# A chain of six layers on one core: gating taken in turn with the next block's top 16, H additions spread, a low rotary product on 128 rows

## The chip, the core and the metric

The kernel runs on one core of a Trainium2 chip. The core has a matrix engine (PE, with PEld for its weight loads), a vector engine (DVE), a scalar engine (ACT), GpSimd (POOL), a queue engine that only issues transfers (SP) and 16 DMA engines. The metric is the device time of one launch in microseconds, as the median of repeated runs: 3226.28 us over 3 runs before the change (3226.07 to 3231.53).

## The reference, cut to what matters

One sequence of 512 tokens (16 meta tokens ahead of it in the first layer) of width 1024, all in float32. The layers in order: a mixer (differential attention beside a gated recurrence), a PEER feed-forward layer, pooling, gated convolution, latent attention (MLA), pooling again, and a last norm. The change is in the mixer's loads, the PEER layer and the MLA layer.

```
# PEER, per block of 128 tokens
q = xb @ w_query                                   # 8 heads, two halves of 128
s = q . subkeys                                    # 128 scores per half
sv, si = top_k(s, 16)                              # "lists": per half the best 16
cand = sv[0][:, None] + sv[1][None, :]             # 256 pairs per head
top_s, pos = top_k(cand, 16)                       # "top 16": the best pairs
experts, gates = i*128 + j of pos, softmax(top_s)
hid = gelu(u_table[experts] . xb) * gates
y = sum of hid * v_table[experts]
# MLA, per head and block of 128 queries
s = (q_nope . k_nope + q_rope . k_rope) * scale, causal softmax, p @ v
```

## The kernel before, in words

Products in full precision are made of three f32r matmuls: each operand is split in a high part (`whi`, `xh`) and a low part (`wlo`, `xl`), and `mm3` (L146 to L149) adds high x high, high x low and low x high. So every weight tile of 128x1024 is loaded by SP (`load_w`, L135), cast to `whi` by ACT (L141) and subtracted to `wlo` by DVE (L143), and then used by 24 matmuls.

The PEER layer does not gather for its first 384 tokens: it computes all 16384 hidden values for them (128 tiles of the table u, 24 matmuls each with 384 columns), multiplies each by a dense gate that is zero for all but the 128 chosen experts, and multiplies with all of the table v (128 tiles again). The last 128 tokens are done by rows: one indirect transfer of POOL (L724) gathers one row of u or v per token, and DVE multiplies it (L737) or adds it (L745); there are 256 such row steps, made by the generator in the class `Few`, three of them fetched ahead.

`peer_early` runs first. For 16 tiles of w_query it makes the scores, and DVE picks the lists (`list_scores`, L788 to L792, in steps). `experts_x` (L799) then scales and splits the input of the u tiles (L803, L219, L220). After that 96 of the 128 u tiles run, one per iteration: `u_tile`, waiting transfers `outs`, the dense matmuls that the iteration before left in `pend`, a row step if one is due, and `some(SIDE)`, which takes steps from the front of the list `side` until their written costs use up SIDE. The list holds DVE work: the rest of the lists, `topk` for the four token blocks (block 3 first, since its experts feed the row steps), and `all_gates`, which builds dense gates for a block of 128 tokens. Gates are made for 8 tokens at a time: two DVE operations of 2048 columns (`oh` L973, `og` L975), 16 small matmuls (L983), and two ACT copies (L986) into `stg`. A `stg` tile holds 32 tokens; there are two of them. When it is full, four transfers of 512 KB to `g_d` are put in `outs`. An iteration issues one of these (L1019), and the function `gates` issues all that wait when it starts on the next 32 tokens (L961, L962). ACT issues them in its own order of work.

`peer_late` runs the other 32 u tiles and all 128 v tiles. It reads the gates back (`get_gates`, L1067), the weighted hidden values are made by DVE (L1054) and split, and `slot` hands out the 208 row steps that are left by a rate per kind of tile (FEW_RATE). A v pass over 8 tiles adds into four PSUM tiles; at its end four DVE additions (L1116) put them into H.

In the MLA layer `unit_a` makes 128 rows of scores of one head by four matmuls: two passes of `qn` x `kn` in float32 (L1458), the f32r product of the stacked rotary query with the high part of the rotary key (L1459), and the product of its high half, 64 rows, with the low part of the key (L1460). The stacked query holds 64 rows of high part and 64 rows of low part, the key's tiles hold the same 64 rows twice. There are 64 such units.

The order of work on each engine inside the PEER layer is the order of the code (`manual_schedule`); engines only wait for each other by semaphores.

## Time and profile before

| | before |
|---|---|
| median of 3 runs | 3226.28 us |
| the profiled execution | 3233.49 us, span 3231.8 us |
| granted PE clock, mean | 0.986 |
| PE busy | 3133.5 us (97%) |
| DVE busy | 2195.7 us (68%) |
| ACT busy | 1191.6 us (37%) |
| POOL busy | 550.1 us (17%) |

Busy time is the time in which an engine has an instruction running. Matmuls overlap in the records, so the mean time of one matmul is longer than the distance to the next: counts over a stretch give the pace. Times of rows are microseconds from the start of the span. In the rows, `mm` is a PSUM tile, `hid` the hidden values of one u tile (one per iteration, so its records mark the iterations), and `row` a gathered row tile.

### The profile page before, as it was taken

Reading aid. Unit: us, or ns where it says so; the run is one execution under the profiler, and the core shown is the slowest. Engines: PE = TensorE matmul, PEld = TensorE weight load, DVE = VectorE, ACT = ScalarE, POOL = GpSimd, SP = SyncE. Lnnn points to the kernel's source line nnn. Section 1 sums busy time; section 2 is a strip of 40 time slices with the busy share of each in tenths; the row PEclk is TensorE's granted clock in tenths of the full one; section 3 lists DMA queues with packets and bytes.
Section 4 is the critical chain, followed back from the end, with each engine's and each line's share of the span. In section 5 each row is a group of like instructions: output and inputs, shape, how many; then the busy total and the mean of one; then the engine's idle time right before and its main releaser. Section 6 shows DMA issues by size and latency. Waiting matters only on the chain.

```text
span 3231.8 us, 42341 instructions
## 1 busy us (share of the span) xinstructions
PE 3133.5 (97%) x16233; PEld 2715.0 (84%) x16233; DVE 2195.7 (68%) x3887; ACT 1191.6 (37%) x1793; POOL 550.1 (17%) x490
## 2 busy tenths in 40 slices
PE   8999999889899999999999999999999999999998
PEld 7787879889899999999988888888888777778886
DVE  5466689989757888888887565544446656666664
ACT  3334323365654233333343223222224444443222
POOL 2121100111114653433350001000002000010001
PEclk9999989999999999999999999999999999999999
DMA  3211225777889999999962333323232222223231
GB/s 115 72 59 33 92 66 175 243 223 242 275 275 327 356 335 353 358 351 341 340 247 92 93 97 93 95 93 97 93 98 65 72 58 71 72 80 96 92 98 65
DMA packets 194395, 525.03 MB, mean 162 GB/s; under 512 B 17040, under 2 KB 71568, under 8 KB 194064
## 3 DMA queue, kind: packets, MB, share of 16 engines
q1 hardware_dynamic: 88128, 300.18, 28.6%
q0 software_dynamic: 38144, 136.33, 11.8%
q10 hardware_dynamic: 67920, 85.82, 7.8%
q8 instruction: 127, 2.08, 0.3%
q14 instruction: 76, 0.62, 0.1%
HBM read 474.03 MB, written 46.14 MB: 161 GB/s over the span
## 4 chain that ended last, share of the span: by engine, by line
PE 66%; issue 15%; DVE 8%; POOL 5%; DMA 4%; ACT 2%; ACTq 0%; POOLq 0%; DVEq 0%
PE mm L147 20%; PE mm L149 19%; PE mm L148 19%; POOL row L724 4%; DMA row<-in_v_rows_dram,gi 2%; DVE wlo L143 2%; DMA hh<-hid_d 1%; PE mm L1491 1%; PE mm L1458 1%; DVE row L737 1%; DVE xg L745 1%; PE mm L438 1%; PE mm L1460 1%; PE mm L1477 1%; PE mm L177 0%
## 5 line engine op out<-in xcount | busy, mean ns | idle before, releaser
L147 PE MATMUL mm<-xh,whi 128*128 128x512 f32 (+2 forms) x2640 | 993.1, 376 | 10.9 <-ACT xh L219 5.9
L149 PE MATMUL mm<-xh,wlo 128*128 128x512 f32 (+2 forms) x2640 | 974.8, 369 | 17.0 <-DVE wlo L143 16.8
L148 PE MATMUL mm<-xl,whi 128*128 128x512 f32 (+2 forms) x2640 | 970.8, 368 | 1.6 <-DVE xl L227 1.4
L141 ACT CAST whi<-wraw 128x1024 fp32r<-128x1024 f32 (+1 forms) x586 | 588.0, 1006 | 1031.9 <-PE mm L148 492.2
L143 DVE TENSOR_TENSOR wlo<-wraw,whi 128x1024 fp32r<-128x1024 f32 (+1 forms) x586 | 686.7, 1173 | 305.9 <-ACT whi L141 303.2
L149 PEld LDWEIGHTS mm<-xh,wlo 128*128 128x128 f32 x2640 | 500.4, 190 | 90.3 <-DVE wlo L143 24.8
L147 PEld LDWEIGHTS mm<-xh,whi 128*128 128x128 f32 x2640 | 500.8, 190 | 82.5 <-ACT xh L219 9.7
L148 PEld LDWEIGHTS mm<-xl,whi 128*128 128x128 f32 x2640 | 500.4, 190 | 68.5 <-DVE xl L227 3.5
L149 PE MATMUL mm<-mh,wlo 128*128 128x384 f32 x1024 | 344.7, 337 | 9.1 <-DVE wlo L143 9.0
L147 PE MATMUL mm<-mh,whi 128*128 128x384 f32 x1024 | 343.1, 335 | 0.5 <-ACT whi L141 0.5
L148 PE MATMUL mm<-ml,whi 128*128 128x384 f32 x1024 | 343.0, 335 | 0.0
L724 POOL DMA_INDIRECT row<-in_u_rows_dram,gi x128 | 176.1, 1376 | 625.4 <-DVE row L737 389.7
L724 POOL DMA_INDIRECT row<-in_v_rows_dram,gi x128 | 176.4, 1378 | 284.1 <-DVE xg L745 248.5
L149 PEld LDWEIGHTS mm<-mh,wlo 128*128 128x128 f32 x1024 | 192.8, 188 | 14.5 <-DVE wlo L143 14.4
L147 PE MATMUL mm<-mxh,whi 128*128 128x512 f32 x512 | 204.4, 401 | 0.0
L148 PE MATMUL mm<-mxl,whi 128*128 128x512 f32 x512 | 202.0, 395 | 0.0
L149 PE MATMUL mm<-mxh,wlo 128*128 128x512 f32 x512 | 201.9, 394 | 0.0
L237 DVE TENSOR_TENSOR H<-H,mm 128x512 f32<-128x512 f32 x144 | 98.8, 686 | 149.4 <-PE mm L149 148.9
L147 PEld LDWEIGHTS mm<-mh,whi 128*128 128x128 f32 x1024 | 192.7, 188 | 0.9 <-ACT whi L141 0.8
L148 PEld LDWEIGHTS mm<-ml,whi 128*128 128x128 f32 x1024 | 192.7, 188 | 0.0
L745 DVE SCALAR_TENSOR_TENSOR xg<-row,actg,xg 128x1024 f32<-128x1024 f32 x127 | 163.7, 1289 | 16.7 <-DMA row<-in_v_rows_dram,gi 15.4
L737 DVE SCALAR_TENSOR_TENSOR row<-row,xg 128x1024 f32<-128x1024 f32 x128 | 154.2, 1218 | 8.7 <-DMA row<-in_u_rows_dram,gi 8.7
(353 smaller groups left out, 3758.5 us busy)
## 6 DMA issues: line engine op xcount, KB each, us to landing
wraw<-in_u_t_dram SPq DMA_DIRECT2D x128, 512.0 KB, 4.3
wraw<-in_v_t_dram SPq DMA_DIRECT2D x128, 512.0 KB, 6.5
wraw<-in_pw_in_dram SPq DMA_DIRECT2D x64, 512.0 KB, 3.5
wraw<-in_cw_in_dram SPq DMA_DIRECT2D x64, 512.0 KB, 3.5
g_d<-stg ACTq DMA_DIRECT2D x48, 512.0 KB, 6.7
g<-g_d ACTq DMA_DIRECT2D x30, 768.0 KB, 6.8
hid_d<-hid ACTq DMA_DIRECT2D x48, 384.0 KB, 4.3
hh<-hid_d ACTq DMA_DIRECT2D x46, 384.0 KB, 6.8
```

Source lines behind the costliest of these rows:

```text
L141: scalar.copy(hi[:, :n], raw[:, :n])
L143: vector.tensor_sub(lo[:, :n], raw[:, :n], hi[:, :n].bitcast(F32))
L147: tensor.matmul(ps, sh, mh, start=start, stop=False)
L148: tensor.matmul(ps, sh, ml, start=False, stop=False)
L149: tensor.matmul(ps, sl, mh, start=False, stop=stop)
L237: vector.tensor_tensor(h[2 * dp + e], h[2 * dp + e], ps, op=OP.add)
L438: tensor.matmul(pl[:, j * 64:(j + 1) * 64].rearrange("p (n b) -> p n b", b=b), kf[:, tiles[j]], pairs_of(q[:, j * 128:(j + 1) * 128], b)[: ...
L724: gpsimd.indirect_dma_start(out=t, out_offset=None, in_=table, in_offset=bass.IndirectOffsetOnAxis(ap=self.gi[:, j:j + 1], axis=0))
L737: vector.scalar_tensor_tensor(t, t, 1.0, self.xg, op0=OP.mult, op1=OP.mult, accum_out=hid[:, j:j + 1])
L745: vector.scalar_tensor_tensor(y, t, act[:, j:j + 1], y, op0=OP.mult, op1=OP.add)
L1458: tensor.matmul(ps[:, :nk], qn[e][:, qs], kn[e][:, :nk], start=True, stop=False)
L1460: tensor.matmul(ps[:, :nk], qr[e][rows, qs], krl[rows, :nk], start=False, stop=True)
```

## The change

Nothing is computed in another way but for one product: `unit_a` now multiplies all 128 rows of the stacked query with the low part of the key, which adds the product low x low that was left out. All else is order.

- `some` keeps a balance: what a step takes beyond its share is taken off the next iteration. SIDE becomes 3.8, less ROW (1.3) for a row step in the same iteration. In the w_query loop it is 4.3 per tile, and nothing after the last tile.
- `both` runs two generators in turn by their written costs; gating of block 0 now goes in turn with `topk(1)`, gating of block 1 with `topk(2)`, with a start of HEAD (11) for the `topk`.
- row steps: one per iteration once the experts are known, until 36 are done, and one per iteration again after the side list is empty. 44 instead of 48 are done in `peer_early`. In `peer_late` the other 212 are due 7 tiles before the end and not 4.
- transfers to `g_d`: an iteration issues two where more than three wait, else one; `gates` only issues what is beyond four.
- the first two reads of the gates in `peer_late` are issued by POOL and not by SP.
- the additions into H are put in a list, and one is made after each of the next weight tiles.
- the mixer loads w_in[17] ahead of the tables of constants.

```
-SIDE = 2.75
+SIDE = 3.8
+SIDE_Q = 4.3
+ROW = 1.3
+HEAD = 11.0
-FEW_EARLY = 48
+FEW_EARLY = 36
...
             pre[12] = load_w(w_in[12])
+            pre[17] = load_w(w_in[17])
...
+        bal = [0.0]
+
         def some(us):
-            while us > 0 and side:
+
+            bal[0] += us
+            while bal[0] > 0 and side:
                 c = next(side[0], None)
                 if c is None:
                     side.pop(0)
                 else:
-                    us -= c
+                    bal[0] -= c
+            bal[0] = min(bal[0], 0.0)
+
+        def both(a, b):
+
+            live = [[HEAD, a], [0.0, b]]
+            while live:
+                g = min(live, key=lambda x: x[0])
+                c = next(g[1], None)
+                if c is None:
+                    live.remove(g)
+                else:
+                    g[0] += c
+                    yield c
...
-            some(4.0)
+            if c < 15:
+                some(SIDE_Q)
...
-            while outs:
+            while len(outs) > 4:
                 scalar.dma_start(*outs.pop(0))
...
-        side += [topk(3), topk(0), topk(1), all_gates(0), topk(2), all_gates(1), all_gates(2)]
+        side += [topk(3), topk(0), both(all_gates(0), topk(1)), both(all_gates(1), topk(2)), all_gates(2)]
...
-            if outs:
+            for _ in range(2 if len(outs) > 3 else 1 if outs else 0):
                 scalar.dma_start(*outs.pop(0))
             for f in now:
                 f()
-            few.upto(min(few.done + 1, int((e + 1) * FEW_EARLY / EARLY)))
-            some(SIDE)
+            was = few.done
+            few.upto(was + 1 if not side else min(was + 1, FEW_EARLY))
+            some(SIDE - ROW * (few.done - was))
...
-        share = (256 - few.done) / sum(FEW_RATE[k] for k in kinds[:-4])
+        share = (256 - few.done) / sum(FEW_RATE[k] for k in kinds[:-7])
...
+        adds = []
+
+        def take_w():
+            w = next_w()
+            if adds:
+                adds.pop(0)()
+            return w
...
         for _ in range(2):
-            get_gates(sync)
+            get_gates(gpsimd)
             get_hid(sync)
...
-                    vector.tensor_tensor(hd, hd, acc[dt][:, :ND], op=OP.add)
+                    adds.append(lambda hd=hd, a=acc[dt][:, :ND]: vector.tensor_tensor(hd, hd, a, op=OP.add))
             parts = coming
+        while adds:
+            adds.pop(0)()
         few.upto(10 ** 6)
...
-                rows = slice((e % 2) * 64, (e % 2) * 64 + 64)
...
-                tensor.matmul(ps[:, :nk], qr[e][rows, qs], krl[rows, :nk], start=False, stop=True)
+                tensor.matmul(ps[:, :nk], qr[e][:, qs], krl[:, :nk], start=False, stop=True)
```

The built programs show how the instructions move. The first place is ACT's order at the first hand-over of gates in the u loop. Before (L141 the weight cast, L1008 one u tile, L986 the copies into `stg`, L962 and L1019 the transfers to `g_d`):

```order
L1008 ACTIVATE hid<-mm 128x384
L1010 DMA hid_d<-hid 128x768
L1019 DMA g_d<-stg 128x8x128
L986 ACTIVATE stg<-mm 128x4x128 x2
L141 CAST whi<-wraw 128x1024
L1008 ACTIVATE hid<-mm 128x384
L1019 DMA g_d<-stg 128x8x128
L986 ACTIVATE stg<-mm 128x4x128 x4
L962 DMA g_d<-stg 128x8x128 x6
L141 CAST whi<-wraw 128x1024
```

The same place of the changed program (L144 the weight cast, L1030 one u tile, L1008 the copies, L1041 the transfers):

```order
L1030 ACTIVATE hid<-mm 128x384
L1032 DMA hid_d<-hid 128x768
L1041 DMA g_d<-stg 128x8x128 x2
L144 CAST whi<-wraw 128x1024
L1030 ACTIVATE hid<-mm 128x384
L1041 DMA g_d<-stg 128x8x128
L1008 ACTIVATE stg<-mm 128x4x128 x2
L144 CAST whi<-wraw 128x1024
L1030 ACTIVATE hid<-mm 128x384
L1032 DMA hid_d<-hid 128x768
L1041 DMA g_d<-stg 128x8x128
```

Six transfers stood in a row ahead of one weight cast, at three places of the loop, and two in a row at two more; now two stand in a row at most, and two of the 48 stand at the end of an iteration, just ahead of its weight cast.

The second place is DVE's order where gating of block 0 begins. Before (L143 the weight's low part, L737 a row step, L903 to L928 the end of `topk(1)`, L973 and L975 the gates):

```order
L928 TENSOR_TENSOR ij<-ij,z 128x128
L953 TENSOR_TENSOR gts<-gf,gts 128x16x8
L973 TENSOR_TENSOR oh<-iotax,keys 128x2048
L143 TENSOR_TENSOR wlo<-wraw,whi 128x1024
L737 SCALAR_TENSOR_TENSOR row,hidg<-row,xg 128x1024
L975 TENSOR_TENSOR og<-oh,gts 128x2048
L973 TENSOR_TENSOR oh<-iotax,keys 128x2048
L975 TENSOR_TENSOR og<-oh,gts 128x2048
L143 TENSOR_TENSOR wlo<-wraw,whi 128x1024
```

Now (L146 the weight's low part, L741 a row step, L902 to L927 parts of `topk(1)`, L995 and L997 the gates):

```order
L146 TENSOR_TENSOR wlo<-wraw,whi 128x1024
L741 SCALAR_TENSOR_TENSOR row,hidg<-row,xg 128x1024
L912 TENSOR_SCALAR acc<-acc 128x128
L913 TENSOR_TENSOR ab<-acc 128x128
L914 TENSOR_SCALAR acc<-acc 128x128
L915 TENSOR_TENSOR ab<-acc 128x128
L997 TENSOR_TENSOR og<-oh,gts 128x2048
L146 TENSOR_TENSOR wlo<-wraw,whi 128x1024
L741 SCALAR_TENSOR_TENSOR row,hidg<-row,xg 128x1024
L925 TENSOR_TENSOR rb<-ab,iotaa 128x1024
L927 TENSOR_TENSOR rb<-rb,sf 128x1024
L995 TENSOR_TENSOR oh<-iotax,keys 128x2048
```

Three gate operations between two weights have become one beside a piece of the next block's top 16. The first gate operation stands at the same weight tile as before; the last of block 0 comes later.

The third place is DVE's order at the end of the first v pass of `peer_late`. Before (L1116 the additions into H):

```order
L737 SCALAR_TENSOR_TENSOR row,hidg<-row,xg 128x1024 x2
L1116 TENSOR_TENSOR H<-H,mm 128x384 x4
L143 TENSOR_TENSOR wlo<-wraw,whi 128x1024
L1054 TENSOR_TENSOR sq<-acc,g 128x384
L220 TENSOR_TENSOR ml<-sq,mh 128x384
```

Now (L1147 the additions into H):

```order
L146 TENSOR_TENSOR wlo<-wraw,whi 128x1024
L1147 TENSOR_TENSOR H<-H,mm 128x384
L1085 TENSOR_TENSOR sq<-acc,g 128x384
L223 TENSOR_TENSOR ml<-sq,mh 128x384
L741 SCALAR_TENSOR_TENSOR row,hidg<-row,xg 128x1024 x2
```

The four additions in one piece ahead of a weight's low part have become single ones, each behind the low part of one of the next four weight tiles.

## Rows read from the trace of the kernel before

**Rows 1.** Busy time by stage: PE, PEld, DVE, ACT, POOL (instructions), clock, DMA
```profile
481.00:987.00 506.00, 464.44 (x3064) 452.74 (x3064) 408.45 (x859) 249.00 (x314) 59.00 (x50) 0.96 0.76 240
987.00:1678.00 691.00, 676.85 (x3850) 667.52 (x3848) 598.39 (x776) 245.21 (x334) 298.82 (x209) 1.00 0.93 341
...
2500.00:2880.00 380.00, 374.74 (x1845) 289.70 (x1844) 228.20 (x516) 167.87 (x363) 29.41 (x30) 1.00 0.25 71
```

**Rows 2.** Timeline of ACT at the end of the 96 u tiles: start, us, instruction [idle before]
```profile
974.69 0.49 ACT L1008 ACTIVATE hid<-mm 128x384 f32<-128x384 f32 x1 [2.19 <-PE mm L149]
...
987.25 0.49 ACT L1008 ACTIVATE hid<-mm 128x384 f32<-128x384 f32 x1 [2.76 <-PE mm L149]
```

**Rows 3.** What PE waited for, 481 to 987: total, times, longest
```profile
PE mm L983 <- DVE og L975: 30.2, 11, 7.2
PE mm L149 <- DVE wlo L143: 11.3, 13, 2.0
```

**Rows 4.** Timeline of all engines around a run of transfers, 688 to 712
```profile
694.57 7.96 ACTq L962 DMA_DIRECT2D g_d<-stg  x4
...
702.57 1.04 ACT L141 CAST whi<-wraw 128x1024 fp32r<-128x1024 f32 x1 [8.03 <-DMA g_d<-stg]
...
707.07 1.22 DVE L973 TENSOR_TENSOR oh<-iotax,keys 128x2048 f16<-128x2048 f16 x1
...
707.22 1.89 PE L983 MATMUL mm<-og,oh 128*128 128x128 f16 x16 [5.93 <-DVE og L975]
```

**Rows 5.** Instructions on `g_d`: ns min/median/max, starts; last, landing
```profile
L1019 ACTq DMA_DIRECT2D g_d<-stg x26: 366/414/1377, 685.8 to 941.2; - x26
L962 ACTq DMA_DIRECT2D g_d<-stg x22: 366/1741/3119, 691.9 to 888.8; - x22
...
DMA to landing us min/median/max: 4.1/6.8/10.4
```

**Rows 6.** Timeline of DVE, 571 to 600
```profile
573.50 1.20 DVE L143 TENSOR_TENSOR wlo<-wraw,whi 128x1024 fp32r<-128x1024 f32 x1
574.62 1.22 DVE L737 SCALAR_TENSOR_TENSOR row<-row,xg 128x1024 f32<-128x1024 f32 x1
...
595.08 1.22 DVE L143 TENSOR_TENSOR wlo<-wraw,whi 128x1024 fp32r<-128x1024 f32 x1
```

**Rows 7.** Timeline around the first u tile, 455 to 486
```profile
455.58 0.29 DVE L788 MAX8 sv<-mm 128x8 f32<-128x128 f32 x1
...
465.10 0.73 DVE L803 SCALAR_TENSOR_TENSOR sq<-H,vc,rb 128x512 f32<-128x512 f32 x1
...
466.43 0.69 PE L147 MATMUL mm<-xh,whi 128*128 128x384 f32 x1 [4.54 <-ACT xh L219]
```

**Rows 8.** Timeline of ACT at the first u tile's end
```profile
480.65 0.49 ACT L1008 ACTIVATE hid<-mm 128x384 f32<-128x384 f32 x1 [0.19 <-PE mm L149]
```

**Rows 9.** What PE waited for, 0 to 60: total, times, longest
```profile
PE mm L149 <- DVE wlo L143: 1.8, 1, 1.8
...
PE mm L147 <- ACT whi L141: 0.9, 1, 0.9
```

**Rows 10.** What PE waited for, 990 to 1690
```profile
PE mm L149 <- DVE wlo L143: 12.7, 21, 2.0
```

**Rows 11.** Timeline of PE in the MLA layer, 2596 to 2603
```profile
2599.81 0.50 PE L1460 MATMUL mm<-krl,qr 64*128 64x512 f32 x1
2600.24 0.51 PE L147 MATMUL mm<-mxh,whi 128*128 128x512 f32 x1
2600.58 0.40 PE L148 MATMUL mm<-mxl,whi 128*128 128x512 f32 x1
2600.82 0.39 PE L149 MATMUL mm<-mxh,wlo 128*128 128x512 f32 x1
```

**Rows 12.** Weight loads (PEld) of the same stretch
```profile
2600.24 0.19 PEld L147 LDWEIGHTS mm<-mxh,whi 128*128 128x128 f32 x1 [0.25 <-issue]
2600.35 0.19 PEld L148 LDWEIGHTS mm<-mxl,whi 128*128 128x128 f32 x1
```

More of the change, by code (lines that the diff above doesn't have):

```diff
@@ L1091, in peer_late @@
                     ps = ptile()
-                    mm_tile(ps[:, :ND], next_w(), 0, xn)
+                    mm_tile(ps[:, :ND], take_w(), 0, xn)
                     a = np_.tile([128, T], F32, name="acc", bufs=2)
@@ L1102, in peer_late @@
                 for q2 in range(8):
-                    w = next_w()
+                    w = take_w()
                     for q in range(2):
```

## The prediction

> **What bounds the kernel now.** I read the stages first [rows 1]. PE is busy for 374.7 of 380 us in the MLA layer and for 676.9 of 691 us in the late PEER stage, at full clock: there PE is the bound, and only what PE itself does, or its few waits, can be saved. In the stretch of the 96 u tiles it is not: of 506 us it is busy for 464.4, at a granted clock of 0.96, so part of the busy time is at the lower level. What one u tile costs PE when nothing disturbs it is read at the end of that stretch: its ACT records lie 12.56 us apart over three tiles, 4.19 us each [rows 2]. A block of 8 gated tokens adds 16 small matmuls: in a quiet place I take 1.0 us, a little over half of the 1.89 us that 16 took just after a stall [rows 4]; 48 of them are 48 us. With 2.5 us of transposes and last scores, PE's floor from the end of the first u tile to the end of the last is 95 x 4.19 + 48 + 2.5 = 448.5 us. The records say 987.25 - 480.65 = 506.6 us [rows 2, 8]. So 58 us are lost there, and the question is what the new order gives back.
>
> The waits name two causes [rows 3]. PE waited 30.2 us for `og`, in 11 pieces of up to 7.2 us, and 11.3 us for `wlo`, in 13 pieces; the rest of the 58 us is slow clock behind these. The first cause is ACT. A run of six transfers stands in ACT's order ahead of a weight cast; the last four took 7.96 us to issue, the cast came 8.03 us late, and PE sat 5.93 us on `og` [rows 4]. A transfer issued alone takes 0.41 us, in such runs 1.74 us, up to 3.1 [rows 5]. Three runs of six stand in the order; at 8 us each plus the clock behind it, I put 26 us on them. The second cause is DVE. Between 573.5 and 595.1 four weight tiles took 21.58 us, 5.40 us each [rows 6], while PE could take one every 4.19 us. PE lives on the three weight tiles made ahead and then falls back to DVE's pace. That is the other 32 us.
>
> **The change, part by part.** The sum is made against the profiled execution, 3233.5 us (span 3231.8); the median of the runs is 3226.3, 7.2 us lower, and I carry the sum over to it.
>
> 1. w_in[17] earlier. PE waits 0.9 and 1.8 us for that tile's `whi` and `wlo` [rows 9]. It is now cast behind four squares on ACT and not behind all eight, and its transfer goes ahead of the tables. Next is w_in[13], whose cast comes right after, and PE then has 48 matmuls to do. Term -2.5, between 0 and -2.7.
>
> 2. Before the u tiles. DVE did six list steps in 465.10 - 455.58 = 9.5 us before it began to scale the input, 1.6 us each, and PE waited 4.54 us for it [rows 7]. By the new order three stand there, so the scaling begins 4.8 us sooner, which is just when PE comes free; the eight scalings behind it keep their own pace. Term -4.5, between -4.8 and 0. The lists left over (26 steps where 17 were) go into the u stretch and are priced there.
>
> 3. The u stretch. I count DVE's order up to the point that the small matmuls behind the 44th u tile need: 42 weights (1.20 us each), 22 row steps (1.22), 6 gate operations (1.22) [rows 4, 6], 26 list steps (1.6) and 225 of the 326 small operations of the top 16. Their price is what DVE's busy time leaves: 408.5 - 96 x 1.2 - 48 x 1.22 - 96 x 1.22 - 17 x 1.6 = 90 us for 326, 0.28 us each [rows 1]. The sum is 50 + 27 + 7 + 42 + 63 = 189 us, with 0.2 us of small waits per weight 197, and DVE starts 3 us behind PE: 200. PE's floor to the same point is 43 x 4.19 + 3 + 2.5 = 186. So DVE still holds PE back by some 14 to 17 us by then. Behind it the two are level (an iteration then carries a weight, a row step, about one gate operation and four small ones of the top 16, 4.7 us by the same prices, against 4.19 + 0.5 on PE), and from the 72nd tile on PE has three gate operations' worth of small matmuls per tile, 5.7 us, against 4.9 on DVE. So DVE's lateness is paid once, where before it was paid in each `topk` anew.
> The runs of six are gone. Two transfers in a row cost ACT some 1.5 us, and ACT is busy for only half of the stretch [rows 1]. A new wait comes in: a `stg` tile is used again every second block of 32, and its transfers, issued later now, need 6.8 us to land [rows 5]. By the order three of the ten re-uses (near tiles 75, 80 and 83) follow the last transfer by less than one tile. ACT then waits some 4 us with a weight cast behind it, for a tile that PE needs two tiles later; 5 us in all for PE. Left of the 58 us: 17 + 5. Term -36. Ends: everything saved, -58; DVE as now and the runs come back as waits on `stg`, -10.
>
> 4. The late stage. PE waits 12.7 us there for `wlo` [rows 10], part of it behind the four H additions in one piece, which hold up the next weight. Spread, each is 0.5 us behind a weight that is already made. Against that, 212 row steps stand in 153 tiles and not 208 in 156: 4% more per tile, 0.05 x 1.2 us more on DVE in each of 153 tiles, 10 us in all, of which DVE's idle 93 us of 691 take most [rows 1]; the DMA engines are at a share of 0.93 with no room to speak of. Term -3, between -10 and +12. The two gate reads on POOL's queue wait for `g_d` there and hold up row fetches only; POOL is idle for more than half of the stage [rows 1].
>
> 5. MLA. The 64-row product takes more of PE than its columns. With 512 columns, L1460 begins at 2599.81, the next matmul 0.43 us later, the one after 0.34 us after that; in undisturbed rows of the same size the distance is 0.24 [rows 11]. That is 0.19 + 0.10 = 0.29 us; a drain ahead of L1460 I put at between 0 and 0.1. The loads show why: the load after L1460 begins with its own matmul at 2600.24, after 0.25 us of nothing, while the next one begins 0.23 us ahead of its matmul [rows 11, 12]. With all 128 rows the product should stand in the stream like any other. Per unit 0.33 us; 64 units, 21 us. PE is the bound here, so it is all on the path; what could be late next is the softmax between units, since each unit is shorter by a twentieth. Term -21, between -25 and 0.
> The Trainium skill speaks on both sides. Its page "TensorE: Matmul & The Clock Gate" (Part 3: Packing small matmuls — row/col tiling) says that a weight load overlaps a running matmul only when its row group differs; by that, full rows gain nothing and this term is 0. The trace disagrees: full 128-row loads run 0.23 us ahead throughout [rows 12]. The Trainium skill's page "TensorEngine Tiling (Array Packing)" (Key Properties) says that a change of tiling mode drains TensorE; by that the term is what rows 11 show.
>
> Sum: -2.5 - 4.5 - 36 - 3 - 21 = -67. From 3233.5 that is 3166.5; from the median 3159.
>
> **The rivals.** A: the hand-over of `stg` stalls again. If ACT's waits for landing reach PE at most re-uses, with 4 us each for ten, 40 us less 5 already counted come back: 3194. For it: 6.8 us of landing against 5.7 us per tile. Against: seven of ten re-uses have two tiles or more.
> B: the late stage becomes bound by its rows. DMA share 0.93 and DVE at 87% leave little; the 10 us of extra DVE work and the DMA's lateness then all fall on PE, and the additions save nothing: +12 for -3, 3174.
> C: the MLA product gains nothing, since the gap belongs to the change of operand type or to the load itself: 3180. Against it: the normal rows next to it. By the Trainium skill's overlap rule, weighed in part 5, this is the outcome.
> D, on the other side: ACT is held at every re-use as it is now in its runs, 8 us (the price of rows 4) at each of ten, and PE starves each time: 80 us, on top of it the clock falls behind each stall. It decides from about 7 us per re-use, since 67 are to be lost: 3159 + 80 = 3239. For it: PE was thrown off by just such waits. Against: no run of more than two is left.
>
> **How the numbers follow.** Forecast 0.62, A 0.12, B 0.13, C 0.08, D 0.05. The predicted time is the forecast's, 3159. Below it, all of the u stretch saved (-22) with the late gain of -10 would be 3130; above it, A is 3194, and B and C lie inside. I take 3130 to 3194 as holding 8 in 10. A measurement of this kernel can tell about 0.2%, 6.5 us, from no change. Slower by more than that needs D in full: 0.05. Within it, parts of D and A together: 0.03. Faster: 0.92.
>
> **What would show it.** In the profile after: PE waits for `og` in the u stretch fall from 30 us to under 12, and no `g_d` run of ACT over 4 us is left; the stretch from first to last u tile is 470 us, give or take 12; the first u tile follows the last scores with no wait over 1 us; L1460's successor begins some 0.23 us behind it at 512 columns and the layer is 21 us shorter; `wlo` waits of the late stage are under 13 us. I am wrong if the u stretch stays over 490 us, if the late stage grows by more than 10 us, or if the 128-row product keeps its gap.

## The result, and the profile after

| | before | after |
|---|---|---|
| median | 3228.91 us (3226.07 to 3232.08) | 3190.23 us (3189.07 to 3192.3) |
| ratio | | 0.9881, 95% interval 0.9864 to 0.9898 |
| the profiled execution | 3233.49 us, span 3231.8 us | 3189.07 us, span 3187.4 us |

The change saves 38.7 us, 44.4 between the two profiled executions; the forecast was 67. The measured 3190 lies inside the range that was given (3130 to 3194), near its upper end. The span is cut at six events: the first copy of a query tile, the start of ACT's first and last gelu of the 96 u tiles, the end of the last late v matmul, and the start of the first and the last matmul of `unit_a` with the high rotary key.

| stretch | before | after | difference | forecast |
|---|---|---|---|---|
| start to first query tile | 366.7 | 364.7 | -2.0 | -2.5 |
| to the first u tile's gelu | 113.9 | 109.2 | -4.7 | -4.5 |
| the u stretch, to the 96th gelu | 506.6 | 471.8 | -34.8 | -36 |
| the late stage | 690.9 | 707.6 | **+16.7** | **-3** |
| to the first MLA unit | 828.9 | 828.9 | 0.0 | 0 |
| the 64 MLA units | 368.3 | 347.8 | -20.5 | -21 |
| to the end | 356.4 | 357.4 | +1.0 | 0 |

Four of the five terms came out within 1.2 us. The late stage did not: it makes up 19.7 of the 22.6 us by which the saving in the profile falls short of the forecast.

Busy time by stage in the changed kernel, as in [rows 1]: u stretch, late stage, MLA.

```profile
474.00:946.00 472.00, 457.92 (x3068) 447.16 (x3069) 416.55 (x924) 249.72 (x315) 51.41 (x49) 0.98 0.77 247
946.00:1654.00 708.00, 686.42 (x3847) 671.43 (x3845) 602.79 (x786) 245.57 (x335) 308.32 (x214) 0.99 0.92 340
2474.00:2834.00 360.00, 354.05 (x1853) 290.22 (x1851) 227.59 (x516) 167.90 (x365) 29.49 (x30) 1.00 0.25 75
```

In the late stage PE is busy for 9.6 us more, with the same matmuls, and idle for 21.6 us where it was 14.2: waits and a clock that fell behind them. DVE's share is lower than before (602.8 of 708 against 598.4 of 691), and so is the DMA share, 0.92. Neither has become a bound over the whole stage; the loss must be read in places.

What PE waited for in the changed kernel: in the u stretch (two lines, against [rows 3]), then in the late stage (three lines, against [rows 10]).

```profile
PE mm L152 <- DVE wlo L146: 8.1, 10, 2.6
PE mm L1005 <- DVE og L997: 5.1, 3, 4.3
...
PE mm L152 <- DVE wlo L146: 11.2, 26, 0.9
PE mm L150 <- ACT whi L144: 5.6, 3, 4.3
PE mm L755 <- DVE xg L749: 3.6, 1, 3.6
```

`og` fell from 30.2 to 5.1 us. Late, two waits that were 0.5 and 0.8 us before stand beside `wlo`: 5.6 us for `whi`, 4.3 of it in one piece, and 3.6 us for `xg`. The first is followed back by the rows around the hand-over, where the last u tile of the early stretch ends (945.70) and the first of the late stage begins. Timelines of ACT (three rows), SP (three) and then DVE and PE, with the idle time before an instruction in brackets:

```profile
924.78 1.70 ACTq L1041 DMA_DIRECT2D g_d<-stg  x1
929.86 0.51 ACTq L1041 DMA_DIRECT2D g_d<-stg  x1
...
957.28 1.04 ACT L144 CAST whi<-wraw 128x1024 fp32r<-128x1024 f32 x1 [11.09 <-DMA wraw<-in_u_t_dram]
...
925.76 7.36 SPq L142 DMA_DIRECT2D wraw<-in_u_t_dram  x3
943.62 0.81 SPq L1103 DMA_DIRECT2D hh<-hid_d  x2
944.52 19.30 SPq L142 DMA_DIRECT2D wraw<-in_u_t_dram  x5
...
958.36 1.23 DVE L146 TENSOR_TENSOR wlo<-wraw,whi 128x1024 fp32r<-128x1024 f32 x1 [13.01 <-ACT whi L144]
...
958.38 0.69 PE L150 MATMUL mm<-xh,whi 128*128 128x384 f32 x1 [4.34 <-ACT whi L144]
```

SP's waits between 900 and 1000:

```profile
SPq L1103 <- DMA g_d<-stg: 10.4, 1, 10.4
```

The last gate write goes out at 929.86 (941.20 before, but there 46 us ahead of the last u tile's gelu [rows 2, 5], here 16 us ahead). The first hid read `hh` is on SP's queue; its tile lies where a `stg` tile lay, so it waits until that write has landed. SP stands 10.4 us on it, and the weight loads stand behind it. Before, a gate read stood ahead of it on the same queue, and the two went out at 974.20 and 974.64 without a wait, for the last gate write had gone out 33 us earlier:

```profile
974.20 0.38 SPq L1067 DMA_DIRECT2D g<-g_d  x1
974.64 0.60 SPq L1072 DMA_DIRECT2D hh<-hid_d  x1
```

Now the next weight is cast 11.1 us late, DVE idles 13.0 us, and PE, after it has used the weights made ahead, 4.3 us.

How far PE falls behind is told by one number: the start of its k-th matmul after the 96th gelu, less k times 0.1744 us, the pace of undisturbed matmuls there (4.19 us for 24 [rows 2]). In us:

| k | place | before | after |
|---|---|---|---|
| 48 | two u tiles in | 0.1 | 5.6 |
| 480 | 16 u tiles and 4 v tiles in | 3.5 | 14.9 |
| 3600 | ten v tiles before the end | 19.8 | 31.0 |
| 3840 | the end | 20.0 | 36.7 |

The first 50 us of the stage (columns as in [rows 1]):

```profile
946.00:996.00 50.00, 44.54 (x235) 42.85 (x234) 31.96 (x50) 16.78 (x28) 20.08 (x15) 0.93 0.86 316
```

So 11.4 us are lost by k = 480, between 480 and 3600 as much as before (16.1 against 16.3), and over the last ten tiles 5.5 more than before, where the wait for `xg` is. PE's granted clock is 0.93 over the 50 us that hold the stall; before it was 1.00. The loss goes on after the stall, and DVE can't make it good beside the late u tiles: a tile with one row step takes it 3.9 us in the timeline, one with two 5.0; at 1.60 on the mean that is 4.6, against PE's 4.19. (With the 1.52 of before it would be 4.5, so there was no room there either.)

46 of the 48 gate writes in the changed kernel (against [rows 5]), their durations min/median/max in ns:

```profile
L1041 ACTq DMA_DIRECT2D g_d<-stg x46: 366/487/1944, 692.3 to 929.9; - x46
```

No run of more than two is left; the longest single issue is 1.94 us where there were 3.12. And PE in an MLA unit of 512 columns, then its loads (against [rows 11, 12]):

```profile
2512.85 1.02 PE L1490 MATMUL mm<-t 128*128 128x512 f32 x2
2513.31 0.80 PE L1491 MATMUL mm<-krh,qr 128*128 128x512 f32 x1
2513.94 0.40 PE L1492 MATMUL mm<-krl,qr 128*128 128x512 f32 x1
2514.18 0.39 PE L150 MATMUL mm<-xh,whi 128*128 128x512 f32 x1
2514.41 0.40 PE L151 MATMUL mm<-xl,whi 128*128 128x512 f32 x1
...
2513.28 0.19 PEld L1491 LDWEIGHTS mm<-krh,qr 128*128 128x128 f32 x1 [0.24 <-issue]
2513.71 0.19 PEld L1492 LDWEIGHTS mm<-krl,qr 128*128 128x128 f32 x1 [0.24 <-issue]
2513.94 0.19 PEld L150 LDWEIGHTS mm<-xh,whi 128*128 128x128 f32 x1
```

In the kernel before, the product ahead of L1460 (2599.81 [rows 11]) began at 2599.09:

```profile
2599.09 0.79 PE L1459 MATMUL mm<-krh,qr 128*128 128x512 f32 x1
```

The successor follows 0.24 us behind L1492 and the next 0.23 behind that, where it was 0.43 and 0.34; the load after L1492 runs ahead of its matmul again.

### The profile page after: what moved, and what is told of

It is laid out like the page before. It is cut to its first block, busy times and chain, and to the rows that moved or that the text cites. A ratio compares the mean times of both kernels' runs of the same rounds, so it can differ in the third digit from the quotient of the medians.

```text
span 3187.4 us, 42357 instructions
## 1 busy us (share of the span) xinstructions
PE 3114.2 (98%) x16233; PEld 2713.7 (85%) x16233; DVE 2194.8 (69%) x3887; ACT 1190.9 (37%) x1793; POOL 551.3 (17%) x492
## 3 DMA queue, kind: packets, MB, share of 16 engines
q0 software_dynamic: 38432, 137.91, 11.9%
## 4 chain that ended last, share of the span: by engine, by line
PE 69%; issue 11%; DVE 8%; POOL 5%; DMA 4%; ACT 2%; ACTq 0%; POOLq 0%; DVEq 0%
PE mm L150 20%; PE mm L152 20%; PE mm L151 20%; POOL row L728 5%; DMA row<-in_v_rows_dram,gi 3%; DVE wlo L146 2%; PE mm L1005 1%; PE mm L1523 1%; PE mm L1490 1%; PE mm L442 1%; DVE row L741 1%; PE mm L180 1%; PE mm L1509 0%; ACT whi L144 0%; DMA g_d<-stg 0%
## 5 line engine op out<-in xcount | busy, mean ns | idle before, releaser
L144 ACT CAST whi<-wraw 128x1024 fp32r<-128x1024 f32 (+1 forms) x586 | 588.7, 1007 | 1011.3 <-PE mm L151 487.9
L146 DVE TENSOR_TENSOR wlo<-wraw,whi 128x1024 fp32r<-128x1024 f32 (+1 forms) x586 | 688.5, 1176 | 292.2 <-ACT whi L144 289.4
L152 PEld LDWEIGHTS mm<-xh,wlo 128*128 128x128 f32 x2640 | 501.6, 190 | 85.8 <-DVE wlo L146 19.7
L152 PEld LDWEIGHTS mm<-mh,wlo 128*128 128x128 f32 x1024 | 192.7, 188 | 16.6 <-DVE wlo L146 16.3
L749 DVE SCALAR_TENSOR_TENSOR xg<-row,actg,xg 128x1024 f32<-128x1024 f32 x127 | 163.5, 1287 | 14.7 <-DMA row<-in_v_rows_dram,gi 13.2
L741 DVE SCALAR_TENSOR_TENSOR row<-row,xg 128x1024 f32<-128x1024 f32 x128 | 154.0, 1220 | 5.7 <-DMA row<-in_u_rows_dram,gi 5.7
```

Of the source, the lines that this page charges most:

```text
L144: scalar.copy(hi[:, :n], raw[:, :n])
L146: vector.tensor_sub(lo[:, :n], raw[:, :n], hi[:, :n].bitcast(F32))
L152: tensor.matmul(ps, sl, mh, start=False, stop=stop)
L741: vector.scalar_tensor_tensor(t, t, 1.0, self.xg, op0=OP.mult, op1=OP.mult, accum_out=hid[:, j:j + 1])
L749: vector.scalar_tensor_tensor(y, t, act[:, j:j + 1], y, op0=OP.mult, op1=OP.add)
```

## The experiments

The medians of the kernel before lay between 3228.8 and 3229.8 us beside all of them. Where an edit is to the changed kernel, its 3190.23 us is what to compare with; the changed kernel itself was not run again beside them. A table behind experiment 12 has the stretches of all of them. The expectations call the experiments by these numbers, e1 to e12.

**1. The MLA product alone, on the kernel before.**

```
-  tensor.matmul(ps[:, :nk], qr[e][rows, qs], krl[rows, :nk], ...)
+  tensor.matmul(ps[:, :nk], qr[e][:, qs], krl[:, :nk], ...)
```

> The kernel before with one edit: the third product of unit_a on all 128 rows. My reading (the 64-row product costs 0.33 us per unit): about 21 us less than before, near 3208, all of it between the first and the last MLA unit (368.3 to about 348 us), every other stretch as before. Rival C (full rows gain nothing): 3229, no change, and the 20.5 us that the MLA layer of the changed kernel gained come from something else, for instance from how the layer is entered.

3211.53 us, 0.9948 (0.9930 to 0.9966), that is 11 to 23 us less. The MLA units take 346.2 us, 22.1 less. Rival C falls. What the run also shows is how much the late stage varies from execution to execution: with the late code of before untouched it took 680.0 us here, 690.9 in the profile of before. (The profiled execution is the fastest of the six.)

**2. The hid reads later on SP's queue.**

```
+  read = lambda t=hq[-1], s=hid_d[hid_of.pop(0)]: eng.dma_start(t, s)
+  read() if eng is scalar else hold.append(read)
   ...
   slot(0)
+  if q > 7 and hold:
+      hold.pop(0)()
```

> The changed kernel, but the two hid reads on SP's queue (hh) are issued behind the 9th and 10th late u tile instead of ahead of the late stage. Theory Q: the late stage lost its 17 us mostly at its start, because the first of these reads stands 10.4 us on SP for the landing of the last gate writes (its tile lies where stg lay), and the weight loads stand behind it. Then PE's 4.3 us wait for whi at the first late u tile and the clock of 0.93 in the first 50 us go, the late stage is 8 to 11 us shorter (707.6 to about 698), and the kernel is near 3181. Theory R (rival B of the prediction: the rows and DMA share bind the stage everywhere): the weights are late anyhow, the late stage stays at 705 to 708 and the time at 3190.

3187.27 us (0.9851 to 0.9894); the late stage 704.7, 2.9 less. Theory Q wanted 8 to 11: it fell short. PE's wait for `whi` is gone (0.1 us behind at k = 48), but at k = 480 PE is still 9.2 us behind. The wait had a successor, seen in what DVE waited for, 945 to 1050 (total, times, longest):

```profile
DVE sq L1085 <- DMA g<-g_d: 7.5, 1, 7.5
```

DVE comes to weight the first late u tile and stands 7.5 us for the gate read on POOL's queue; the next weights are behind it. POOL had waited 4.0 us for the same last write before it could issue that read:

```profile
946.46 1.14 POOL L1098 DMA_DIRECT2D g<-g_d  x2 [3.96 <-DMA g_d<-stg]
```

Without this edit the late code of the changed kernel takes as little in another run (704.5 in experiment 10), so the trace shows where the wait went, but not that anything was saved.

**3. Row steps over 156 tiles.** `kinds[:-7]` back to `kinds[:-4]`.

> The changed kernel, with the 212 late row steps handed out over 156 tiles (kinds[:-4]) and not over 153. Theory R (rows bind the late stage): the steps per tile fall by 2%, DVE has about 4 us less ahead of each point in the stage, the late stage is 4 to 8 us shorter and the kernel near 3184. Theory Q: only the last wait for xg changes (3.6 us at 30 us before the end, of which 2 to 3 us can go), the start of the stage is as it was; late stage 704 to 708, 3187 to 3190.

3179.80 us (0.9828 to 0.9865), 10 less than the changed kernel. But in the profiled execution the late stage is only 1.4 us shorter, 706.2; that execution took 3186.4 us, and the other four 3178.5 to 3180.0. So the number helps, more than theory Q allowed, and this trace can't show where. PE's wait for `xg` is 2.3 us there, where it was 3.6.

**4. The H additions in one piece again.**

```
-  if adds:
-      adds.pop(0)()
   ...
   adds.append(lambda ...)
+  while adds:
+      adds.pop(0)()
```

> The changed kernel, with the four H additions at the end of each half in one piece again, as in the kernel before. If spreading them saves what the prediction said, the late waits for wlo come back in some of the 16 places (up to 2 us each) and the late stage is 3 to 8 us longer, 3193 to 3198. If holding the four PSUM tiles longer is what the late stage lost (a rival for its 17 us), it is 5 to 15 us shorter, 3175 to 3185. Theory Q: the loss is at the start, which this doesn't touch; change within 5 us either way.

3195.93 us (0.9882 to 0.9922), 5.7 more; the late stage 711.9, 4.3 more. PE's waits in the late stage:

```profile
PE mm L152 <- DVE wlo L146: 20.0, 32, 2.7
```

20.0 us for `wlo` against 11.2, with pieces of up to 2.7 us against 0.9: spreading the additions takes these waits away, as it was said to, and is not where the 17 us went. How much time it saves is less sure: the medians' intervals overlap, and 711.9 is only 0.5 us more than the late code took in experiment 8 without this edit.

**5. Last writes sooner.** Experiment 2, and two writes per tile once the side work is used up.

```
-  for _ in range(2 if len(outs) > 3 else 1 if outs else 0):
+  for _ in range(2 if len(outs) > 3 or outs[1:] and not side else 1 if outs else 0):
```

> e2_hidread_later with one more edit: once the side work is used up, two gate writes are issued per u tile, so the last one goes out one tile sooner. Theory H (DVE and the weights lose at the hand-over whatever the last gate writes hold up; in e2 it is DVE itself, 7.5 us on the first g): the last write lands some 4 us sooner, DVE's wait for g falls from 7.5 to about 3.5, the loss of PE in the first 480 matmuls of the late stage falls from 9.2 to about 6, near 3184. Theory R (only the rate of row steps binds): as e2, 3187.

3184.18 us (0.9841 to 0.9874), the time that was expected, but not by the way that was expected: DVE still waits 6.1 us for `g`, and PE is 9.1 us behind at k = 480. This time the gate reads themselves waited for no write:

```profile
944.23 1.18 POOL L1098 DMA_DIRECT2D g<-g_d  x2
```

So what DVE waits for here is the read's own time in flight, and not the last gate write. The late stage is 705.6. The difference of 3 us from experiment 2 isn't settled by this pair.

**6. Side work faster.** One number in the changed kernel: SIDE 4.2 for 3.8. The last gate write now goes out eight u tiles sooner.

> The changed kernel with one number changed: SIDE 4.2 for 3.8, so that the side work ends 8 u tiles sooner and the last gate write stands behind tile 83 and not 91, 34 us sooner. Theory H: the first hid read and the first gate reads wait for nothing, the weight loads go on, and PE loses about 4 us in the first 480 matmuls of the late stage where it lost 14.9: late stage 697 or less, the u stretch 472 (470 to 480, since DVE has more per tile in front and less behind), the kernel 3178 to 3184. Theory R: the late stage stays at 705 or more and the kernel at 3188 or more.

3194.65 us (0.9877 to 0.9910): 4.4 slower than the changed kernel, so the time was missed. At the hand-over it went as expected: PE is 0.1 us behind at k = 48 and 4.9 at k = 480, the late stage is 696.3. That is 11.3 less, and the 10.0 by k = 480 are nearly all of it. No read at the hand-over waits any more. (Row steps follow the side work, so 52 of them are done ahead of the late stage and not 44; 29 stand in the first 480 matmuls where 30 stood, so that is not what the 10.0 come from.) But the u stretch grew from 471.8 to 490.5. What PE waited for there:

```profile
PE mm L152 <- DVE wlo L146: 16.3, 19, 2.6
PE mm L1005 <- DVE og L997: 9.5, 7, 3.1
```

Both waits about doubled: DVE can't do the side work faster without being late with the weights. So the two stretches have to be added. The u stretch and what is lost after it by k = 480 come to 506.6 + 3.5 = 510.1 us before, 471.8 + 14.9 = 486.7 in the changed kernel and 490.5 + 4.9 = 495.4 here.

**7. All mends together, SIDE 4.0.** Experiments 2, 3 and 5, and SIDE 4.0.

> All that should mend the late stage together: hid reads later (e2), last writes sooner (e5), SIDE 4.0, and the row steps over 156 tiles (e3). If the hand-over costs 11 us and the row rate 5 to 10, and they add: 3189 less 16 to 21, near 3171, late stage 686 to 692. If they are one and the same lateness of DVE: as the better of them alone, near 3179.

3183.61 us (0.9841 to 0.9874). The late stage is 687.5, as expected (686 to 692), with 3.7 us lost at k = 480; the u stretch is 490.2, which was not expected. (DVE still waits 4.2 us for the first `g`; with the weights made ahead PE doesn't feel it.) Against experiment 6 the late stage is 8.8 us shorter with little lost at either start; 4.5 of the 8.8 are in the last ten tiles. The number of row steps per tile is not what differs: 48 steps are done early here and 52 there, so the late stage has 208 over 156 tiles here and 204 over 153 there, 1.33 each. What differs is where they end, 15 us before the end of the stage here and 29 there. PE's waits for `xg`, first in experiment 6, then here:

```profile
PE mm L755 <- DVE xg L749: 3.7, 1, 3.7
```

```profile
PE mm L755 <- DVE xg L749: 0.7, 1, 0.7
```

**8. Gate writes issued as before.**

```
-  while len(outs) > 4:
+  while outs:
   ...
-  for _ in range(2 if len(outs) > 3 else 1 if outs else 0):
+  for _ in range(1 if outs else 0):
```

> The changed kernel with the issue of gate writes as before: one per u tile, and all that are left at the next block. By the order ACT then has five runs ahead of a weight cast (4, 4, 6, 4 and 6 transfers). If such runs cost what the prediction put on them (26 us for three of six), the u stretch grows from 472 to between 490 and 505, PE's waits for og come back above 15 us. If the gain of the u stretch came from the new order of the lists and gates alone, it stays within 472 to 480. The late stage begins with the last write two tiles later than in the changed kernel, up to 8 us more there.

3222.06 us (0.9963 to 0.9989). The u stretch is 506.8 us: all of its gain is gone, 35 us, with runs of four to six writes back in ACT's order. The late stage is 711.4, 3.8 more (up to 8 was expected). PE's wait for `og` and ACT's for its own writes:

```profile
PE mm L1005 <- DVE og L997: 29.6, 11, 6.5
...
ACT whi L144 <- DMA g_d<-stg: 22.7, 3, 7.9
```

**9. The first weightings three tiles behind.** Experiment 5 with 3, and for the first four late u tiles:

```
+  if n == 0 and q < 4:
+      a = hq[q // 2][:, q % 2]
   ...
+  wait.append((a, q))
+  for _ in range(min(len(wait), 2 if n or q > 2 else 0)):
+      a, qq = wait.pop(0)
+      parts += gated([a], qq)
```

> e5_writes_sooner with the row steps over 156 tiles (e3) and the weighting of the first four late u tiles three tiles behind their gelu (kept in the two hid tiles, which stand empty there), so that DVE makes three more weights before it needs the first g. SIDE stays at 3.8. Theory H (the hand-over is one stall of DVE, whichever wait it stands in): DVE's 6 to 7 us wait for g goes, PE loses 4 us in the first 480 matmuls as in e7, and the u stretch stays at 471: late stage 688 to 694, kernel 3168 to 3174. If DVE's lateness comes from the u stretch itself and the wait only shows it: late stage 700 or more, 3180 or more.

3176.56 us (3172.85 to 3184.59), 0.9836 (0.9817 to 0.9855): the fastest of all, and 13.7 us below the changed kernel (its interval overlaps that of experiment 3, which is part of it). It is still not what was expected: the profiled execution has a late stage of 705.5 us, which the expectation gave to the other reading. The wait for `g` is gone, and the u stretch is 472.2, but PE is 9.6 us behind at k = 480, for DVE waits for a row:

```profile
957.46 1.23 DVE L741 SCALAR_TENSOR_TENSOR row<-row,xg 128x1024 f32<-128x1024 f32 x1 [5.66 <-DMA row<-in_u_rows_dram,gi]
```

That row was fetched 12.1 us earlier, right behind the two gate reads of 768 KB each, neither of which waited for a write:

```profile
943.84 1.18 POOL L1098 DMA_DIRECT2D g<-g_d  x2
945.34 1.74 POOL L728 DMA_INDIRECT row<-in_u_rows_dram,gi  x1 [0.32 <-DVE row L741]
```

So after SP on `hh` and DVE on `g` this is a third place where DVE and the weights stop at the hand-over, but neither here nor in experiment 5 does anything wait for the last gate write. What all of them share is the load: over the 20 us ahead of the 96th gelu the DMA share is 1.02 in the changed kernel, 1.06, 1.05 and 1.04 in experiments 2, 5 and 9, and 0.89 before, 0.97 and 0.82 in experiments 6 and 7. The other reading, that DVE comes late out of the u stretch, finds no support: over the same 20 us DVE is busy for only 13.0 us in the changed kernel and 11.5 here, and what it waits for is the next weight's cast or a row. No run took load off the DMA engines alone, so that cause stays argued. The profiled execution is the slowest of its five, so where the gain of the median sits isn't shown.

**10. Gate blocks and top 16 one after the other.**

```
-  side += [topk(3), topk(0), both(all_gates(0), topk(1)), both(all_gates(1), topk(2)), all_gates(2)]
+  side += [topk(3), topk(0), topk(1), all_gates(0), topk(2), all_gates(1), all_gates(2)]
```

> The changed kernel with the gate blocks and the top 16 one after the other, as before (no both), still dosed by the balance. The prediction gave DVE's order about 10 of the 36 us in the u stretch. If that holds, the u stretch is 478 to 486 us, with waits for wlo behind each top 16 and for og behind the gates, kernel 3196 to 3204. If the transfer runs were all of it (e8 gave back 35), 470 to 475 and 3188 to 3192.

3193.63 us (0.9873 to 0.9914). The u stretch is 479.5 us, 7.7 more: taking the two in turn is worth that, near the 10 that the prediction put on DVE's order. The median is only 3.4 us higher, less than the 6 to 14 that were expected, and its interval overlaps that of the changed kernel.

**11. Other row rates on top of 9.** FEW_RATE (1.1, 1.7, 0.3).

> e9_gates_behind with other row rates (1.1, 1.7, 0.3 for 1.3, 1.6, 0.3): fewer row steps beside the late u tiles, where a tile takes DVE 4.5 us against PE's 4.19, more beside the v tiles. If DVE is what PE waits for beside the u tiles: the 3.5 and 5 us that PE loses in those two stretches shrink to under 2 each, 3 to 6 us less than e9. If the DMA engines bind the v tiles (share 0.95 to 1.00 there): what is saved is lost there again, within 2 us of e9.

3184.77 us (0.9845 to 0.9880), 8.2 more than experiment 9, though its profiled late stage is 2.5 us shorter (703.0) and PE only 4.7 us behind at k = 480. At the end of the 16 v tiles that follow the first 16 u tiles (k = 768) it is 8.1 us behind, against 9.4 in experiment 9: most of what was saved beside the u tiles was lost beside the v tiles. Why the median is higher is open.

**12. The new issue of writes alone, on the kernel before.** The two lines of experiment 8 the other way round.

> The kernel before with one thing changed: how gate writes are issued (two per u tile while more than three wait, and a block starts with up to four left). Lists, dosing, row steps, H additions and MLA are as before. If the runs of transfers were the whole of what the u stretch lost and gave (e8): the stretch falls from 506.6 to about 472, and since the side work ends 10 tiles before the stretch does, no hand-over stall comes: near 3194. If the order and the dosing of the lists are needed too: 485 to 500, 3207 to 3222.

3212.67 us (0.9927 to 0.9961). The u stretch is 493.2, 13.4 less than before, and `og` still costs 17.2 us. The late stage takes 684.1 with the old late code. So issue and dosing need each other: 13 us for the issue alone, 35 for both, and by experiment 8 nothing for the dosing without the issue.

The stretches of all profiled executions, with what PE loses in the late stage by k = 480, from there to k = 3600, and over the last ten tiles, in us:

| run | u stretch | late stage | by 480 | to 3600 | last ten tiles |
|---|---|---|---|---|---|
| before | 506.6 | 690.9 | 3.5 | 16.3 | 0.2 |
| after | 471.8 | 707.6 | 14.9 | 16.1 | 5.7 |
| 1 | 505.8 | 680.0 | 3.6 | 4.9 | 0.6 |
| 2 | 471.8 | 704.7 | 9.2 | 20.0 | 4.6 |
| 3 | 471.4 | 706.2 | 13.5 | 18.5 | 3.3 |
| 4 | 472.0 | 711.9 | 13.2 | 23.6 | 4.2 |
| 5 | 471.4 | 705.6 | 9.1 | 21.2 | 4.4 |
| 6 | 490.5 | 696.3 | 4.9 | 15.7 | 4.8 |
| 7 | 490.2 | 687.5 | 3.7 | 12.6 | 0.3 |
| 8 | 506.8 | 711.4 | 12.9 | 22.6 | 5.0 |
| 9 | 472.2 | 705.5 | 9.6 | 20.1 | 5.2 |
| 10 | 479.5 | 704.5 | 11.9 | 16.4 | 5.3 |
| 11 | 472.8 | 703.0 | 4.7 | 22.9 | 5.2 |
| 12 | 493.2 | 684.1 | 3.1 | 9.8 | 0.3 |

The u stretch repeats: the changed kernel and the six experiments that leave its order as it is, but for the last writes, lie within 471.4 and 472.8. The late stage does not. The old late code took 680.0 to 690.9 (before, 1, 12), the new one 704.5 to 711.4 (after, 8, 10). So it is clear that the new one is slower, but of the edits made for it only experiments 6 and 7 leave that band by more than 2 us, and the others have only their medians to speak for them.

## Why the prediction was right where it was, and wrong in the late stage

Term 1 (w_in[17], -2.5) measured -2.0, and term 2 (lists before the u tiles, -4.5) measured -4.7; PE's longest wait before the first u tile is 0.6 us, where it was 4.54 [rows 7]. PE's two waits for w_in[17] (0.9 and 1.8 us [rows 9]) are gone.

Term 3, the u stretch, -36: measured -34.8, and its first signs came true (`og` 5.1 us, below 12; no run over 4 us). Its two causes were named rightly, but they do not add as the prediction had it, with 26 us for the runs and the other 10 for DVE's order. The issue alone gives 13 us (experiment 12), taking the lists in turn 8 (experiment 10), and without the new issue the rest gives nothing (experiment 8), where ACT's trace has runs of four or more writes ahead of a weight cast at six places, and before had them at three. So it is partly luck that -36 came out. Part of the gain was also borrowed: the last gate write now goes out behind tile 92 and not 85, and the late stage pays for it; experiments 6 and 7, which end it sooner, have a u stretch longer by 18 to 19 us.

Term 4, the late stage, is the step that failed: forecast -3, at most +12, measured +16.7. By the prediction's own sign ("if the late stage grows by more than 10 us") it is wrong there. The additions do take away `wlo` waits (experiment 4). What failed is the hand-over. "The two gate reads on POOL's queue wait for `g_d` there and hold up row fetches only": the prediction looked at POOL's queue, and neither at what the move left first on SP's nor at how late the last gate write had become, 16 us ahead of the 96th gelu where it was 46. On SP the first hid read waited for that landing, 10.4 us, with the weights behind it, and PE lost 11.4 us more than before by k = 480. Taking SP's wait away (experiment 2) brings the 14.9 us there down to 9.2; in experiments 5 and 9 nothing waits for a gate write any more, and 9.1 and 9.6 remain, with transfers that take long beside DMA engines at a share of 1.0. Where the writes end six to eight tiles sooner, in experiments 6 and 7, the loss falls to 4.9 and 3.7. In experiment 11, with the hand-over of 9 but 25 row steps in the first 480 matmuls and not 30, it is 4.7. So the late end of the side work is shown to cost, and by one pair of runs the row steps beside the first tiles too; how the loss is shared between the wait for the landing, the load of the DMA engines and the row steps stays open.

The second part of term 4 is the row steps: the prediction counted 10 us of DVE work that "DVE's idle 93 us of 691 take most". Over the last ten tiles PE loses 5.5 us more than before. By the table, the four runs with 208 steps over 156 tiles (before, 1, 7 and 12) lose 0.2 to 0.6 there and all others 3.3 to 5.7, also those that end at the same tile with 212 steps (experiments 3, 9 and 11) and the one with the same number per tile (experiment 6). So the hand-out of the rows matters there, and neither where it ends nor how dense it is explains it alone; that cause stays open. Rival B named the rows, at +12 for the stage; the hand-over was no rival's.

The prediction's sign for it ("`wlo` waits of the late stage are under 13 us") came true, 11.2, and said nothing: the time went into `whi`, `xg`, many waits too short for that view, and a slower clock, 0.93 in the 50 us that hold the stall (1.00 in experiment 2, where PE does not stop there).

Term 5, MLA, -21: measured -20.5, and -22.1 alone (experiment 1). The gap ahead of the product, which the prediction put at up to 0.1 us, was there too: it began 0.72 us behind the product ahead of it before, and 0.63 now. The rule of the Trainium skill that the prediction weighed (the page "TensorE: Matmul & The Clock Gate", Part 3: Packing small matmuls — row/col tiling: a load overlaps a running matmul only when its row group differs) would have given nothing here; the measurement decides for the trace's rows.

Rival A and rival D, ACT held at the re-uses of `stg`: ACT waited 5.7 us in all for those landings, 2.7 at most. That the measured time lies near rival A's 3194 is chance. Term by term the profile gives -2.0 - 4.7 - 34.8 + 16.7 - 20.5 + 1.0 = -44.3, the difference of the two spans but for rounding. The medians differ by 5.7 less, since the profiled execution of before lay 4.6 above its median and that of after 1.2 below.

## What to carry to other kernels

When a change moves a read from one queue to another, look at the instruction that is now first on the queue it left: it can meet the same wait, and everything behind it is held. Side work that is dosed to fill a stretch exactly ends in the next one's first loads; leave time between its last write and the hand-over, or add the two stretches up. When a wait is taken away and the time stays, look for its successor on the next engine, and look again at what that one waits for: here SP stood on a late write, DVE on a read that in part had waited for it, and then DVE on a read and on a row that had waited for none. And find out how far a stage repeats with the same code before a few microseconds are read from one pair of traces.

## What the runs showed of the hardware that was not expected

- The same late stage, with the same code, took 690.9, 680.0 and 684.1 us in three profiled executions (before, experiments 1 and 12). The u stretch, with the same order of work, repeated within 1.4 us in seven.
- The score matmuls of a unit are still not at the stream's pace. The load of L1491 begins 0.03 us ahead of its matmul, after 0.24 us of nothing, and L1492 follows 0.63 us behind L1491, where matmuls of the same columns in the stream are 0.23 apart. What it takes to mend that wasn't tried.
- Where the DMA engines were at a share of 0.98 to 1.04 (915 to 945 us in experiment 7, 897 to 922 in experiment 6, 925.7 to 945.7 in the changed kernel), gate writes took longer to land: 13.8 us from issue (929.86) to the release of the read that waited for it (943.62) in the changed kernel, at most 15.5 in experiment 6 and 20.4 in experiment 7, where the longest landing before was 10.4 [rows 5].
